# Two spacer tiles of a hybrid-layer kernel made 32 bytes smaller

## The chip, the cores and the metric

The kernel runs on one core of one Trainium2 chip. The metric is the device time in microseconds. The time before is the median of three runs; profiles are of one execution, whose span (first to last instruction) and own time are given apart.

## The reference

One layer of a streaming encoder on 256 positions of width 2048, in float32. Three sub-layers add to the residual x, each on a modulated RMS norm whose shift, scale and gate come from a vector c:

```python
h = modulate(rms_norm(x, ffn1_norm[l]), sh1, sc1)
x = x + HALF_STEP * g1[:, None, :] * swiglu(h, ffn1_w1[l], ffn1_w3[l], ffn1_w2[l])
h = modulate(rms_norm(x, mix_norm[l]), sh2, sc2)
x = x + g2[:, None, :] * hybrid_mixer(h, w_in[l], ...)
h = modulate(rms_norm(x, ffn2_norm[l]), sh3, sc3)
x = x + HALF_STEP * g3[:, None, :] * swiglu(h, ffn2_w1[l], ffn2_w3[l], ffn2_w2[l])
...
return modulate(rms_norm(x, final_norm), sh_f, sc_f)
```

`swiglu` is `(silu(h @ w1) * (h @ w3)) @ w2` with 5632 hidden columns. `hybrid_mixer` projects h by one matrix of 12,288 columns into a gated convolution branch (31 taps, layer norm), a retention branch (4 heads with q, k of 256 and v of 512 columns, decay, group norm, swish gate) and two gates, and merges the branches. Almost all of the work is matrix products with weights that are each used once.

## The kernel before

Everything is kept transposed: features lie on the 128 partitions, the 256 positions along the free axis. A float32 number is held as two halves in the type float32r, a rounded high half and the low rest. A product of two such numbers is three matmuls: high by high, high by low, low by high. This holds for the weights (tiles `hi` and `lo`) and for the activations (h, s, r2, z, mg2, each with a high and a low half behind one another).

**Weights.** `prep` (L178 to L198) loads a block of up to 1 MB into one of four buffers `raw` by a DMA on SyncE's queue. ScalarE copies a half block into `hi` (L189, five buffers), VectorE subtracts to get `lo` (L192, five buffers). `gemm` (L206 to L219) then runs the products of an output tile: for each 128 x 128 block of weights, which is the stationary operand, one matmul of 256 columns with the high half of the activation and one with the low half (L216, `ps<-h,hi` where h is the moving operand), and after those of a half block the low weights by the high activation (L218). Each matmul has its own weight load, which TensorE carries out while the matmul before it runs. Where six banks are filled side by side (the first part of each feed-forward block and of the mixer), `mm3` (L200 to L204) does the same block by block on three lines. Only `value` (L523 to L538) turns this round: there a 128-column slice of h is stationary, and 512 columns of `hi` or `lo` are the moving operand.

**Order of the work.** First feed-forward block: 24 of 44 hidden tiles with h as the moving operand, in four sets, while h is still being made (L390 to L418); then the rest by `ffn` (L342): a stretch with h as the moving operand, then one with the hidden activations s (`s2` tiles), twice over. Then the mixer: q, k and convolution tiles from h, four heads, each with scores, outputs and `value`; then the gates, W_o with r2 as the moving operand, the pointwise convolution with z, the merged projection with mg2. Then the second feed-forward block. Between the parts a norm needs the whole of x, so TensorE pauses. VectorE also reduces the modulation rows (L110) between the weights.

**Where tiles lie.** Tiles of a pool lie behind one another in each partition's memory, in the order in which their names first come up. Pool `keep` comes first, with h at its start, then pool `wp` with `raw`, the weight halves and the spacers, then the pools of the stages. `apart` (L92 to L96) makes a tile of a given number of bytes once per name, and GpSimd clears it; nothing reads it. The spacers are `apart_w` (L187, 64 bytes) between `raw` and `hi`, `apart_s` (L191, 192 bytes) behind `lo`, and in the mixer's first pool `apart_k` (L579, 64 bytes) between q and k and `apart_p` (L551, 192 bytes) between v and p.

All blocks of `hi`, `lo`, h and the other activations are multiples of 512 bytes long, so what is left of an address modulo 256 is set by the spacers and a few small tiles. From the start of h to `hi` there are 99,136 bytes (h 32,768; the vectors 2176; x 16,384; ones 512; cb 8192; small tiles 704, 128, 256, 32 and 32; ssq 2048; three tiles of 1024; `raw` 32,768; `apart_w` 64), which is 64 modulo 256: h lies 192 beyond `hi` and `lo`. The five buffers of `hi`, the five of `lo` and `apart_s` take 40,960 + 192 bytes, so what begins behind them (s, z, r2, mg2, q) lies 192 beyond `hi` as well. k lies 64 beyond q, so q lies 192 beyond k; p lies 192 beyond v. In `value`, where the operands change places, the moving `hi` lies 64 beyond the stationary h.

In front of each product, then, the moving operand's address is 192 more than the stationary one's, modulo 256, except in `value`.

Of the kernel before, what the change touches and what calls it, by code (L numbers as in the profile page):

```python
# [52 lines left out]
def hybrid_layer(ctx, tc, xT, c, vecs, rope, decay, adaT, w13, w13s, w13t, mixs, w2g, w_ab, w_qk, w_v, w_g,  # L53
# [7 lines left out]
    wp = ctx.enter_context(tc.tile_pool(name="wp", bufs=1))  # L61
# [30 lines left out]
    def apart(pool, name, n):  # L92

        if name not in set_apart:
            set_apart.add(name)
            nc.gpsimd.memset(pool.tile([P, n // 4], F32, name=name, tag=name, bufs=1), 0.0)  # L96
# [3 lines left out]
    def raw_load(src, n):  # L100
        r = wp.tile([P, 2048], F32, name="raw", tag="raw", bufs=RAW)
        nc.sync.dma_start(r[:, :n], src)
        return r
# [49 lines left out]
    def tick():  # L153
        ada_done()
        credit[0] += rate["ada"]
        if credit[0] >= 1.0:
            credit[0] -= 1.0
            ada_ahead()
        taps_credit[0] += rate["taps"]
        while taps_credit[0] >= 1.0:  # L160
            taps_credit[0] -= 1.0
            if taps:
                taps.pop(0)()
        due = []
        for e in later:
            e[0] -= 1
            if e[0] <= 0:
                due.append(e)
        for e in due:
            later.remove(e)  # L170
            e[1]()
# [6 lines left out]
    def prep(src, nk, w, ticks=True):  # L178

        n = nk * w  # L180
        r = raw_load(src, n)
        hk = (nk + 1) // 2
        got = []
        for k0 in range(0, nk, hk):
            k1 = min(nk, k0 + hk)
            c0, c1 = k0 * w, k1 * w
            apart(wp, "apart_w", 64)  # L187
            hi = wp.tile([P, 1024], F32R, name="hi", tag="hi", bufs=HI)
            A.copy(hi[:, :c1 - c0], r[:, c0:c1])  # L189
            lo = wp.tile([P, 1024], F32R, name="lo", tag="lo", bufs=LO)  # L190
            apart(wp, "apart_s", 192)  # L191
            V.tensor_tensor(lo[:, :c1 - c0], r[:, c0:c1], hi[:, :c1 - c0].bitcast(F32), op=ALU.subtract)  # L192
            for k in range(k0, k1):
                b = slice((k - k0) * w, (k - k0 + 1) * w)
                got.append((hi[:, b], lo[:, b], hi))
        if ticks:
            tick()
        return got  # L198
# [126 lines left out]
    def side_by_side(srcs, h, ks, banks, ticks=True):  # L325

        for i, k in enumerate(ks):
            w = prep(srcs[k], 2 * S0, P, ticks)
            across(w, h[k], banks, i == 0, i == len(ks) - 1)
# [12 lines left out]
    def ffn(pool, i, h, s, store):  # L342

        f0 = 0
        for g, n in enumerate(GROUPS):
            last = g == len(GROUPS) - 1
            for f in range(f0 + len(s), f0 + n):
                ps = pair([lambda u=u: prep(w13[i, u, f], ND, P) for u in range(2)], h)
                s.append(hidden(pool, two(ps)))
            st = Stream(pool, half_g[:, i])  # L350
            cuts = [0, n] if n <= ND else [0, n // 2, n]
            for t in range(0, ND, 2):
                if last and t == ND - 4:
                    table(AF.Abs_reciprocal_sqrt)
                    ada_until(9 if i else 3)
                    ada_done()
                    rate["ada"] = 0.0
                ada_until(8 if i else 2, t + 1)
                if last:
                    ada_until(10 if i else 4, t + 1)  # L360
                ps = pair([lambda u=u: [e for a, b in zip(cuts, cuts[1:])
                                        for e in prep(w2g[i][g][t + u, :, a * P:b * P], b - a, P)]
                           for u in range(2)], s)
                st.add(t, ps, last, last and store)
            f0 += n
            s = []
        return st
# [401 lines left out]
```

## Time and profile before

| | |
|---|---|
| median of 3 runs | 2292.61 us (2267.69 to 2320.36) |
| the profiled execution's own time | 2288.67 us |
| its span | 2286.9 us |
| mean granted TensorE clock | 0.995 |
| read from HBM | 609.77 MB, 268 GB/s over the span (with what is written) |
| instructions | 44,559 |

In the lines of the profile, PE is TensorE's matmuls, PEld its weight loads, DVE VectorE, ACT ScalarE, POOL GpSimd. A group's line gives the line of the kernel, the engine and the operation, the tile written and the tiles read, the shape and the count, then the busy time in us, the mean duration of one in ns, and the idle time of the engine in front of them with what ended it. Matmuls overlap, so a duration of 277 ns does not mean that one begins every 277 ns. A row of the table of stretches gives the stretch in us, its length, the time TensorE was busy in it with the number of matmuls that touch it, the granted clock, the DMA engines' busy share and GB/s. A row of the timeline gives start, duration, and in brackets the idle time ahead with what ended it.

### The profile page before, as it was taken

Reading aid. Unit: us, or ns where it says so; the run is one execution under the profiler, and the core shown is the slowest. Engines: PE = TensorE matmul, PEld = TensorE weight load, DVE = VectorE, ACT = ScalarE, POOL = GpSimd, SP = SyncE. Lnnn points to the kernel's source line nnn. Section 1 sums busy time; section 2 is a strip of 40 time slices with the busy share of each in tenths; the row PEclk is TensorE's granted clock in tenths of the full one; section 3 lists DMA queues with packets and bytes.
Section 4 is the critical chain, followed back from the end, with each engine's and each line's share of the span. In section 5 each row is a group of like instructions: output and inputs, shape, how many; then the busy total and the mean of one; then the engine's idle time right before and its main releaser. Section 6 shows DMA issues by size and latency. Waiting matters only on the chain.

```text
span 2286.9 us, 44559 instructions
## 1 busy us (share of the span) xinstructions
PE 2248.2 (98%) x19036; PEld 2221.7 (97%) x19036; DVE 1760.4 (77%) x2212; ACT 1067.3 (47%) x1367; POOL 0.6 (0%) x8
## 2 busy tenths in 40 slices
PE   7999999999999999999999999999999999999997
PEld 5999999999999999999999999999999999999997
DVE  7899887778778669898998788777766666666664
ACT  6544653334444644545544644446544443344443
POOL 0000000000000000000000000000000000000000
PEclk9999999999999999999999999999999999999999
DMA  9999689989888465555777698976877777777762
GB/s 344 349 330 326 221 293 319 332 329 349 311 320 330 155 226 204 175 176 180 253 258 273 224 349 321 339 278 230 292 260 257 269 255 268 272 275 266 250 250 83
DMA packets 92217, 616.86 MB, mean 270 GB/s; under 512 B 10225, under 2 KB 10481, under 8 KB 34673
## 3 DMA queue, kind: packets, MB, share of 16 engines
q1 hardware_dynamic: 90290, 609.81, 74.1%
q10 hardware_dynamic: 1728, 4.20, 0.5%
q8 instruction: 149, 2.44, 0.4%
q14 instruction: 50, 0.41, 0.0%
HBM read 609.77 MB, written 4.19 MB: 268 GB/s over the span
## 4 chain that ended last, share of the span: by engine, by line
PE 95%; DVE 2%; DMA 1%; ACT 1%; issue 0%; DVEq 0%; ACTq 0%
PE ps L216 50%; PE ps L218 25%; PE ps L202 7%; PE ps L203 7%; PE ps L204 6%; DMA raw<-in_adaT 1%; DMA raw<-in_w13s 1%; DVE lo L192 0%; DVE raw L110 0%; DVE f L671 0%; DVE part L416 0%; DVE ssq L272 0%; ACT hi L189 0%; ACT L245 0%; ACT L238 0%
## 5 line engine op out<-in xcount | busy, mean ns | idle before, releaser
L189 ACT CAST hi<-raw 128x1024 fp32r<-128x1024 f32 (+2 forms) x864 | 843.9, 986 | 1116.3 <-PE ps L216 595.4
L192 DVE TENSOR_TENSOR lo<-raw,hi 128x1024 fp32r<-128x1024 f32 (+2 forms) x864 | 978.5, 1142 | 450.0 <-ACT hi L189 429.6
L216 PE MATMUL ps<-h,hi 128*128 128x256 f32 x5888 | 733.5, 277 | 0.0
L216 PEld LDWEIGHTS ps<-h,hi 128*128 128x128 f32 x5888 | 700.3, 188 | 0.2
L110 DVE CUSTOM_DVE_ANT_0 raw<-raw,cb,vec 128x2048 f32<-128x2048 f32 x176 | 412.6, 2345 | 2.6 <-DMA raw<-in_adaT 2.6
L218 PE MATMUL ps<-h,lo 128*128 128x256 f32 x2944 | 396.4, 277 | 0.0
L218 PEld LDWEIGHTS ps<-h,lo 128*128 128x128 f32 x2944 | 363.8, 188 | 0.0
L216 PE MATMUL ps<-s,hi 128*128 128x256 f32 x2816 | 356.7, 279 | 0.0
L216 PEld LDWEIGHTS ps<-s,hi 128*128 128x128 f32 x2816 | 339.3, 188 | 0.0
L202 PE MATMUL ps<-h,hi 128*128 128x256 f32 x1152 | 315.0, 281 | 14.0 <-ACT h L305 13.8
L203 PE MATMUL ps<-h,hi 128*128 128x256 f32 x1152 | 319.9, 280 | 3.9 <-DVE h L308 3.9
L204 PE MATMUL ps<-h,lo 128*128 128x256 f32 x1152 | 317.1, 280 | 0.0
L202 PEld LDWEIGHTS ps<-h,hi 128*128 128x128 f32 x1152 | 216.5, 191 | 16.1 <-ACT h L305 15.3
L203 PEld LDWEIGHTS ps<-h,hi 128*128 128x128 f32 x1152 | 219.8, 191 | 4.5 <-DVE h L308 4.4
L204 PEld LDWEIGHTS ps<-h,lo 128*128 128x128 f32 x1152 | 218.9, 191 | 0.0
L218 PE MATMUL ps<-s,lo 128*128 128x256 f32 x1408 | 193.9, 279 | 0.0
L218 PEld LDWEIGHTS ps<-s,lo 128*128 128x128 f32 x1408 | 176.9, 189 | 0.0
L443 DVE SCALAR_TENSOR_TENSOR acc<-y,vec,acc 128x256 f32<-128x256 f32 x240 | 114.0, 480 | 2.7
L216 PE MATMUL ps<-r,hi 128*128 128x256 f32 x512 | 63.6, 276 | 0.0
L216 PE MATMUL ps<-mg,hi 128*128 128x256 f32 x512 | 63.4, 276 | 0.0
L216 PEld LDWEIGHTS ps<-r,hi 128*128 128x128 f32 x512 | 60.5, 188 | 0.0
L216 PEld LDWEIGHTS ps<-mg,hi 128*128 128x128 f32 x512 | 60.5, 188 | 0.0
(152 smaller groups left out, 1171.6 us busy)
## 6 DMA issues: line engine op xcount, KB each, us to landing
raw<-in_adaT SPq DMA_DIRECT2D x176, 1024.0 KB, 5.9
raw<-in_w SPq DMA_DIRECT2D x148, 1024.0 KB, 5.6
raw<-in_w SPq DMA_DIRECT2D x64, 896.0 KB, 5.7
raw<-in_w13s SPq DMA_DIRECT2D x64, 768.0 KB, 6.1
raw<-in_w_v SPq DMA_DIRECT2D x16, 1024.0 KB, 4.8
raw<-in_w_g SPq DMA_DIRECT2D x16, 1024.0 KB, 4.9
raw<-in_w_gr SPq DMA_DIRECT2D x16, 1024.0 KB, 5.0
raw<-in_w_o SPq DMA_DIRECT2D x16, 1024.0 KB, 5.2
```

The costliest lines, as they stand in the source:

```text
L110: tc.keep_in_program_order(V.tensor_tensor_reduce(r, r, cb, 1.0, vec[:, b:b + 1], op0=ALU.mult, op1=ALU.add, accum_out=mod[:, j, t:t + 1]))
L189: A.copy(hi[:, :c1 - c0], r[:, c0:c1])
L192: V.tensor_tensor(lo[:, :c1 - c0], r[:, c0:c1], hi[:, :c1 - c0].bitcast(F32), op=ALU.subtract)
L202: PE.matmul(o, st[0], mv[0], start=start, stop=False, skip_group_check=skip)
L203: PE.matmul(o, st[0], mv[1], start=False, stop=False, skip_group_check=skip)
L204: PE.matmul(o, st[1], mv[0], start=False, stop=stop, skip_group_check=skip)
L216: PE.matmul(o, w[k][0], mv[k][:, half], start=k == 0 and half == 0, stop=False)
L218: PE.matmul(o, w[k][1], mv[k][:, 0], start=False, stop=k == n - 1)
L443: tc.keep_in_program_order(V.scalar_tensor_tensor(out=acc[:, t], in0=y[:, t, k:k + T], scalar=vec[:, dw + k:dw + k + 1], in1=acc[:, t], op ...
```

## The change

Two spacers become 32 bytes smaller:

```diff
-            apart(wp, "apart_w", 64)
+            apart(wp, "apart_w", 32)
             hi = wp.tile([P, 1024], F32R, name="hi", tag="hi", bufs=HI)
             A.copy(hi[:, :c1 - c0], r[:, c0:c1])
             lo = wp.tile([P, 1024], F32R, name="lo", tag="lo", bufs=LO)
-            apart(wp, "apart_s", 192)
+            apart(wp, "apart_s", 160)
```

`hi` and `lo` move down by 32 bytes and everything behind `apart_s` by 64. h stays: it now lies 224 bytes beyond the weights' halves, modulo 256. s, z, r2, mg2 and q lie 160 beyond them. In `value` the moving `hi` lies 32 beyond the stationary h. q and k, and v and p, move together, and their 192 stays. No instruction is added or taken away.

## The prediction

> **What bounds the kernel now.** I read the page's busy line first, then the chain that ended last, then the costliest groups.
>
> ```profile
> PE 2248.2 (98%) x19036; PEld 2221.7 (97%) x19036; DVE 1760.4 (77%) x2212; ACT 1067.3 (47%) x1367; POOL 0.6 (0%) x8
> ...
> PE 95%; DVE 2%; DMA 1%; ACT 1%; issue 0%; DVEq 0%; ACTq 0%
> ...
> L189 ACT CAST hi<-raw 128x1024 fp32r<-128x1024 f32 (+2 forms) x864 | 843.9, 986 | 1116.3 <-PE ps L216 595.4
> L192 DVE TENSOR_TENSOR lo<-raw,hi 128x1024 fp32r<-128x1024 f32 (+2 forms) x864 | 978.5, 1142 | 450.0 <-ACT hi L189 429.6
> ```
>
> TensorE is busy 98% of the span and holds 95% of the chain. The two halvings that feed it (L189, L192) wait for it, ACT for 595.4 us on L216 alone. So TensorE's stream of weight load and matmul sets the end, and what counts is its pace: the time from one matmul's start to the next.
>
> The second question is which matmuls meet which spacing. These are the groups by line:
>
> ```profile
> L216 PE MATMUL ps<-h,hi 128*128 128x256 f32 x5888 | 733.5, 277 | 0.0
> ...
> L218 PE MATMUL ps<-h,lo 128*128 128x256 f32 x2944 | 396.4, 277 | 0.0
> ...
> L216 PE MATMUL ps<-s,hi 128*128 128x256 f32 x2816 | 356.7, 279 | 0.0
> ...
> L203 PE MATMUL ps<-h,hi 128*128 128x256 f32 x1152 | 319.9, 280 | 3.9 <-DVE h L308 3.9
> L204 PE MATMUL ps<-h,lo 128*128 128x256 f32 x1152 | 317.1, 280 | 0.0
> L202 PE MATMUL ps<-h,hi 128*128 128x256 f32 x1152 | 315.0, 281 | 14.0 <-ACT h L305 13.8 <-ACT h L311 0.2
> ...
> L218 PE MATMUL ps<-s,lo 128*128 128x256 f32 x1408 | 193.9, 279 | 0.0
> ...
> L216 PE MATMUL ps<-r,hi 128*128 128x256 f32 x512 | 63.6, 276 | 0.0
> L216 PE MATMUL ps<-mg,hi 128*128 128x256 f32 x512 | 63.4, 276 | 0.0
> ...
> L203 PE MATMUL ps<-lo,h 128*128 128x512 f32 x128 | 50.8, 397 | 0.0
> ```
>
> With moving operand h: 5888 + 2944 + 3 x 1152 = 12,288. With s: 2816 + 1408 = 4224; r and mg 768 each (512 and half as many lo), z 384: together 6144. So 18,432 matmuls of 256 columns change their spacing. The value projection is apart: 3 x 128 = 384 matmuls of 512 columns, h stationary and hi or lo moving.
>
> The third view is the one that decides: how many matmuls fall into a stretch without idle time, by stage.
>
> ```profile
> core 0: us, PE busy (x), PEclk, DMA share, GB/s
> 100.00:225.00 125.00, 125.00 (x1105) 1.00 0.91 330
> 227.00:337.00 110.00, 110.00 (x936) 1.00 0.73 253
> 341.00:495.00 154.00, 154.00 (x1309) 1.00 0.91 327
> ...
> 782.00:842.00 60.00, 60.00 (x532) 1.00 0.66 220
> 846.00:864.00 18.00, 18.00 (x80) 1.00 0.64 225
> ...
> 1460.00:1540.00 80.00, 80.00 (x708) 1.00 0.85 312
> 1600.00:1840.00 240.00, 240.00 (x2120) 1.00 0.75 268
> 1880.00:2000.00 120.00, 120.00 (x1062) 1.00 0.77 273
> ```
>
> A matmul that straddles an edge is counted, so I take two off each count (one or two for the 512-column row). 100 to 225 us gives 125,000/1103 = 113.3 ns; 1600 to 1840 gives 113.3; s from 1880 gives 113.2; mg from 1460 gives 113.3. But 227 to 337, also h, gives 110,000/934 = 117.8 ns, and s from 341 gives 117.8. The granted clock is 1.00 in all of them. **There are two paces for the same instruction, shape and spacing: 113.3 and 117.8 ns.** I call them the lower and the upper rung. What moves the stream from one to the other is in the timeline:
>
> ```profile
> 225.75 0.28 PE L204 MATMUL ps<-h,lo 128*128 128x256 f32 x1
> 226.25 0.39 PE L202 MATMUL ps<-h,hi 128*128 128x256 f32 x1 [0.22 <-ACT h L311]
> ```
>
> One stall of a fraction of a microsecond, and the upper rung stands from there through h, s, h and s until the next pause:
>
> ```profile
> core 0: us, PE busy (x), PEclk, DMA share, GB/s
> 227.00:768.00 541.00, 541.00 (x4595) 1.00 0.84 306
> ...
> 1280.00:1543.00 263.00, 263.00 (x2323) 1.00 0.85 312
> 1557.00:2270.00 713.00, 713.00 (x6294) 1.00 0.71 255
> ```
>
> The DMA share is 0.84 on the upper rung and 0.91 or 0.71 on the lower, so neither clock nor DMA load is the cause; what the rows leave is how the weight load's reads and the moving operand's reads fall relative to each other. That is a reading of these rows, not something that one of them shows directly.
>
> From the rungs follow two fixed points. The 4593 matmuls of the upper stretch cost 4.5 ns each over the lower rung, 21 us: a run wholly on the lower rung would be 2288.7 - 21 = 2268 us, and the fastest of the three runs is 2267.69. All 18,432 on the upper rung would be 2268 + 83 = 2351; the slowest run, 2320.36, lies between. The spread of before is then about which rung a run falls on. My sums start from the profiled execution (span 2286.9, its time 2288.67), which is 4 us under the median of 2292.61.
>
> **The change part by part.** Two memsets get shorter:
>
> ```profile
> L96 POOL MEMSET apart_w<- x1: 111/111/111, 0.7 to 0.7; 128x16 f32 x1
> L96 POOL MEMSET apart_s<- x1: 138/138/138, 0.8 to 0.8; 128x48 f32 x1
> ```
>
> They run in the first microsecond on an engine busy for 0.6 us in all, before TensorE has an operand; if nothing hid them they would be worth under 0.3 us. No instruction, transfer or wait is added or removed, and no buffer count changes. Everything rests on addresses.
>
> ACT's and DVE's tiles shift too, in 864 copies and 864 subtractions. The rows of L189 and L192 bound this: ACT waits 1116 us and DVE 450 us ahead of them, so even 10% on each (84 and 98 us) stays inside that slack. I take 0.
>
> Not touched are the head's own products: k sits behind its spacer of 64 and p behind its spacer of 192, both unchanged, so q against k and p against v keep their 192.
>
> For the rest no row shows a matmul at 224 or 160. The nearest rows are the spacing 192 itself, and the value projection, whose moving hi lies 64 beyond its stationary h. The row from 846 to 864 gives 18,000/78.5 = 229 ns for 512 columns. To compare, I need what 256 columns cost when nothing is held up. The nearest is a weight load whose neighbour has no matmul streaming yet:
>
> ```profile
> 33.73 0.19 PEld L203 LDWEIGHTS ps<-h,hi 128*128 128x128 f32 x1 [1.33 <-DVE h L308]
> 33.84 0.19 PEld L204 LDWEIGHTS ps<-h,lo 128*128 128x128 f32 x1
> 33.96 0.19 PEld L202 LDWEIGHTS ps<-h,hi 128*128 128x128 f32 x1
> ```
>
> The first gap is 0.11 us, the next, with matmuls running, 0.12. I take 110 ns as the unheld pace of load and 256 columns (an estimate; the view rounds to 10 ns). A 512-column matmul at 64 is then held for 229 - 220 = 9 ns, a 256-column one at 192 for 114.4 on average (3.3 or 7.8 by rung, a quarter of the matmuls on the upper) - 110 = 4.4. So spacing matters, and 64 is the worse by 4.7 ns a matmul.
>
> On a circle of 256 bytes, 192 and 64 are opposite; 224 and 160 both lie 32 of 128 bytes on the way from the one to the other. My value is a quarter of the difference, 1.2 ns on each of 18,432 matmuls, +22 us: **2288.7 + 22 = 2311 us**. In terms of rungs it says that half of the matmuls run on the upper instead of a quarter. The bounds: never held, -4.4 ns (-81 us); as badly held as at 64, +4.7 ns (+87 us); the class with h twice as heavy as the other. The value projection goes from 64 to 32: 384 matmuls, between all its hold gone (-3 us) and as much again (+3); I take 0, as both ends are small.
>
> A rule of the Trainium skill speaks against any effect. "TensorE: Matmul & The Clock Gate", section "Part 2: What happens when you issue a matmul", gives TensorE two independent read ports and says that loading the next weights takes nothing from the running matmul. By it, the sum would be 0 and the time 2289. The two paces at one clock do not bear it out as it stands, though they do not show the ports either.
>
> **The rivals.**
>
> *Nothing happens* (the paces do not depend on a 32-byte shift): rungs and odds as now, 2289 us, anywhere from 2268 to 2320. For it: 4593 matmuls in a row stayed on one rung through changes of tile, slot and load. Against it: 229 ns at spacing 64. The same holds if spacers are rounded up to a coarser grain when memory is laid out, since the change would then not do what it says. The port rule of the Trainium skill above is this case too.
>
> *Slower: a third rung becomes the standing one.* One matmul shows it:
>
> ```profile
> 1556.27 0.29 PE L204 MATMUL ps<-h,lo 128*128 128x256 f32 x1
> 1556.40 0.28 PE L202 MATMUL ps<-h,hi 128*128 128x256 f32 x1
> ```
>
> Here the gap is 0.13 us, about one step above the upper rung (117.8 + 4.5 = 122 ns, an estimate that fits the row). If h at 224 locks there, 12,288 x (122 - 114.4) = 93 us: 2382 us; s, r, mg and z at 160 alone would add 47 (2336), both 140 (2429). A hold as at 64 for all gives 2376, so I price the case at 2380. It decides from a mean pace of 117.1 ns on (2338 us). For it: the rungs are evenly spaced, and the next one is visited. Against: at 192 it is left at once.
>
> *Faster: the reads stop meeting.* All at 110 ns: 2288.7 - 81 = 2208 us; h alone -54 (2235), the 160 class alone -27 (2262). For it: the bare load shows that the floor is there, 3.3 ns under the lower rung. Against: no long stretch of the trace stands on it.
>
> **How the numbers follow.** Forecast 0.36, with its own range 2268 to 2351; nothing happens 0.14; slower 0.32; faster 0.18. A measurement of this kernel tells about 2% from no change: below 2247 or above 2338. Of the forecast 0.04 lies above 2338; of the faster case 0.02 (the 160 class alone) lies within. So faster 0.16, same 0.32 + 0.14 + 0.02 = 0.48, slower 0.32 + 0.04 = 0.36. The range goes from all reads apart, 2208, rounded to 2205, to a little above the slower case's 2380, at 2400; both classes on the third rung (2429) is left out.
>
> **What would show it right or wrong.** The stretches of the table, counted again, should give paces between 113 and 118 ns, h and s stretches not alike, and the same clock; L216 on h should have a mean above 277 ns if its share of the upper rung grows. The value projection should move by a few ns from 229. All of it is wrong if stages without idle time show paces of 110 ns or under, or of 122 and over, for a whole stage; if the paces are unchanged but idle time ahead of PE grows (over the 14.0 and 3.9 us of L202 and L203), the address story itself is wrong, and the feeding engines were the ones that changed.

## The result and the profile after

The changed kernel takes 2356.2 us (median of 4 runs, 2355.19 to 2356.44) against 2306.49 for the kernel before in the same comparison (4 runs, 2267.69 to 2322.88): a ratio of 1.0305, 95% interval 1.025 to 1.036. The ratio goes by fast runs alone, without those of before that lie more than 1.5% above its fastest; the plain medians are 2.2% apart. It is slower: its fastest run lies above every run of before, here and in the comparisons below. It is also steadier: its four runs lie within 1.3 us, those of before within 55.

The page of the changed kernel, the lines that answer to those shown of before (its span is 2353.4 us, the profiled execution's time 2355.19):

```profile
PE 2315.4 (98%) x19036; PEld 2287.5 (97%) x19036; DVE 1764.5 (75%) x2212; ACT 1071.4 (46%) x1367; POOL 0.6 (0%) x8
...
PE 97%; DVE 1%; ACT 1%; issue 0%; DVEq 0%
...
L189 ACT CAST hi<-raw 128x1024 fp32r<-128x1024 f32 (+2 forms) x864 | 846.6, 986 | 1183.0 <-PE ps L216 728.3
L192 DVE TENSOR_TENSOR lo<-raw,hi 128x1024 fp32r<-128x1024 f32 (+2 forms) x864 | 981.1, 1143 | 503.6 <-ACT hi L189 485.7
L216 PE MATMUL ps<-h,hi 128*128 128x256 f32 x5888 | 757.1, 281 | 0.0
...
L202 PE MATMUL ps<-h,hi 128*128 128x256 f32 x1152 | 319.2, 285 | 13.8 <-ACT h L305 13.8
L203 PE MATMUL ps<-h,hi 128*128 128x256 f32 x1152 | 324.1, 284 | 3.5 <-DVE h L308 3.5
```

The instruction counts are the same. One ScalarE copy takes 986 ns as before, one subtraction 1143 against 1142; ScalarE waits longer, for TensorE above all (L216, 728.3 us against 595.4), and VectorE behind it. TensorE's idle time (span less busy) is 38.0 us against 38.7. All of the 66.5 us is in TensorE's busy time: the same matmuls follow one another more slowly. The mean duration of L216 on h went from 277 to 281 ns.

The table of stretches of the changed kernel, each stretch with one class of matmul and no idle time (in this order: h, s, h, value, mg, h, s, h, s):

```profile
core 0: us, PE busy (x), PEclk, DMA share, GB/s
35.00:346.00 311.00, 311.00 (x2626) 1.00 0.84 300
349.00:504.00 155.00, 155.00 (x1324) 1.00 0.91 333
507.00:685.00 178.00, 178.00 (x1506) 1.00 0.87 321
...
856.00:875.00 19.00, 19.00 (x83) 1.00 0.63 218
...
1493.00:1580.00 87.00, 87.00 (x744) 1.00 0.80 296
1589.00:1906.00 317.00, 317.00 (x2674) 1.00 0.71 255
1909.00:2063.00 154.00, 154.00 (x1315) 1.00 0.75 265
2066.00:2245.00 179.00, 179.00 (x1515) 1.00 0.71 252
2248.00:2336.00 88.00, 88.00 (x744) 1.00 0.44 152
```

And three stretches of the kernel before with nearly the same counts (mg, h, s):

```profile
1459.00:1543.00 84.00, 84.00 (x744) 1.00 0.83 307
1552.00:1856.00 304.00, 304.00 (x2667) 0.99 0.74 264
...
2186.00:2270.00 84.00, 84.00 (x744) 1.00 0.44 158
```

Two off each count again for the edges. With h at 224 the pace is 118.3 ns (178,000/1504 = 118.4, 179,000/1513 = 118.3; the two longer stretches, which begin just behind a pause, give 118.5 and 118.6). Neither 113.3 nor 117.8 is left. With the rest at 160 there are two paces: 117.3 (349 to 504, 1493 to 1580, 1909 to 2063) and 118.7 (the last, 88,000/742 = 118.6). The last row of both shows the loss plainly: 744 matmuls of s in 84 us before, 88 after, at the same clock and the same DMA share. The value projection goes from 229 to 19,000/81.5 = 233 ns.

Over all 18,432 matmuls the mean pace went from 114.4 to 118.1 ns: 3.7 x 18,432 = 68 us, and 384 x 4 ns = 2 us in the value projection, against 66.5 measured; a tenth of a nanosecond in the paces is 2 us.

### The profile page after: what moved, and what is told of

It reads as the page before. It is cut to its first block, busy times and chain, and to the rows that moved or that the text cites. A ratio compares the mean times of both kernels' runs of the same rounds, so it can differ in the third digit from the quotient of the medians.

```text
span 2353.4 us, 44559 instructions
## 1 busy us (share of the span) xinstructions
PE 2315.4 (98%) x19036; PEld 2287.5 (97%) x19036; DVE 1764.5 (75%) x2212; ACT 1071.4 (46%) x1367; POOL 0.6 (0%) x8
## 4 chain that ended last, share of the span: by engine, by line
PE 97%; DVE 1%; ACT 1%; issue 0%; DVEq 0%
PE ps L216 50%; PE ps L218 25%; PE ps L202 7%; PE ps L203 7%; PE ps L204 7%; DVE f L671 0%; DVE ssq L272 0%; ACT L245 0%; ACT L238 0%; DVE lo L192 0%; PE gn_v L256 0%; PE gn_m L256 0%; DVE raw L110 0%; ACT sq L288 0%; PE r L256 0%
## 5 line engine op out<-in xcount | busy, mean ns | idle before, releaser
L189 ACT CAST hi<-raw 128x1024 fp32r<-128x1024 f32 (+2 forms) x864 | 846.6, 986 | 1183.0 <-PE ps L216 728.3
L192 DVE TENSOR_TENSOR lo<-raw,hi 128x1024 fp32r<-128x1024 f32 (+2 forms) x864 | 981.1, 1143 | 503.6 <-ACT hi L189 485.7
L216 PE MATMUL ps<-h,hi 128*128 128x256 f32 x5888 | 757.1, 281 | 0.0
L216 PEld LDWEIGHTS ps<-h,hi 128*128 128x128 f32 x5888 | 722.4, 188 | 0.2
L218 PE MATMUL ps<-h,lo 128*128 128x256 f32 x2944 | 408.2, 281 | 0.0
L218 PEld LDWEIGHTS ps<-h,lo 128*128 128x128 f32 x2944 | 373.8, 188 | 0.0
L216 PE MATMUL ps<-s,hi 128*128 128x256 f32 x2816 | 362.2, 280 | 0.0
L216 PEld LDWEIGHTS ps<-s,hi 128*128 128x128 f32 x2816 | 344.6, 188 | 0.0
L202 PE MATMUL ps<-h,hi 128*128 128x256 f32 x1152 | 319.2, 285 | 13.8 <-ACT h L305 13.8
L203 PE MATMUL ps<-h,hi 128*128 128x256 f32 x1152 | 324.1, 284 | 3.5 <-DVE h L308 3.5
L204 PE MATMUL ps<-h,lo 128*128 128x256 f32 x1152 | 321.0, 283 | 0.0
L202 PEld LDWEIGHTS ps<-h,hi 128*128 128x128 f32 x1152 | 217.1, 192 | 15.5 <-ACT h L305 15.3
L203 PEld LDWEIGHTS ps<-h,hi 128*128 128x128 f32 x1152 | 219.9, 191 | 4.2 <-DVE h L308 4.0
L204 PEld LDWEIGHTS ps<-h,lo 128*128 128x128 f32 x1152 | 218.4, 191 | 0.0
L216 PE MATMUL ps<-r,hi 128*128 128x256 f32 x512 | 66.2, 281 | 0.0
L216 PE MATMUL ps<-mg,hi 128*128 128x256 f32 x512 | 65.4, 280 | 0.0
L216 PEld LDWEIGHTS ps<-r,hi 128*128 128x128 f32 x512 | 63.0, 189 | 0.0
L216 PEld LDWEIGHTS ps<-mg,hi 128*128 128x128 f32 x512 | 62.4, 188 | 0.0
```

The source lines that it names most:

```text
L202: PE.matmul(o, st[0], mv[0], start=start, stop=False, skip_group_check=skip)
L203: PE.matmul(o, st[0], mv[1], start=False, stop=False, skip_group_check=skip)
L204: PE.matmul(o, st[1], mv[0], start=False, stop=stop, skip_group_check=skip)
L216: PE.matmul(o, w[k][0], mv[k][:, half], start=k == 0 and half == 0, stop=False)
L218: PE.matmul(o, w[k][1], mv[k][:, 0], start=False, stop=k == n - 1)
```

## The experiments

### Each part alone, the parts swapped, everything moved

**h at 224 alone.** Only the first spacer shrinks.

```diff
-            apart(wp, "apart_w", 64)
+            apart(wp, "apart_w", 32)
```

> apart_w 32 and apart_s 192: h 224 beyond the weights' halves, everything behind apart_s back at 192. If the spacing of a product's two operands sets its pace (theory S): stages with h at 118.3 ns a matmul as after the change, stages with s, r2, z and mg2 on the two rungs of before (113.3 or 117.8 ns); time 2268 + 12288 x 5.0 ns = 2329 us with the rest on the lower rung, up to 2357 on the upper. If the place of the weights' halves itself is what counts (theory P: they lie where they lie after the change): both classes as after, 2353 us, s at 117.4.

2340.97 us (4 runs); ratio to before 1.0243, interval 1.017 to 1.0316 (before in this and the next three: 2280.98, 19 runs, 2267.14 to 2321.21). Its stretches of h, s, s:

```profile
35.00:346.00 311.00, 311.00 (x2626) 1.00 0.84 300
349.00:504.00 155.00, 155.00 (x1319) 1.00 0.91 325
...
689.00:773.00 84.00, 84.00 (x744) 1.00 0.83 302
```

h has the row of the changed kernel to the last digit. s, back at 192, shows both rungs of before, 117.7 and 113.2 ns. The halves lie where they lie after the change, and s does not mind: it is the spacing, not the place.

**The rest at 160 alone.**

```diff
-            apart(wp, "apart_s", 192)
+            apart(wp, "apart_s", 160)
```

> apart_w 64 and apart_s 160: h at 192, the rest at 160. Theory S: h stages at 113.3 or 117.8 ns by chance, s, r2, z and mg2 at 117.3 to 118.5 whatever the rung before them; time 2268 + 6144 x 4.3 ns = 2294 us with h wholly on the lower rung, up to 2349. Theory P (the halves lie as before the change): both classes on the two rungs, 2268 to 2350 with stretches of 113.3 in s stages.

2307.91 us (10 runs); 1.011, interval 1.0065 to 1.0155. Stretches of h, s, h, s:

```profile
507.00:685.00 178.00, 178.00 (x1514) 1.00 0.87 322
688.00:776.00 88.00, 88.00 (x744) 1.00 0.79 288
...
2039.00:2210.00 171.00, 171.00 (x1511) 1.00 0.73 262
2213.00:2300.00 87.00, 87.00 (x743) 1.00 0.43 151
```

h at 192 is on the upper rung (117.7) in the first pair and on the lower (113.3) in the second, and s follows: 118.6 after the upper, 117.4 after the lower. So s at 160 also has two paces, both above 117, and in this run they go with the rung that h leaves. That is not all that decides: in the changed kernel both paces of s stand behind h at 118.3. The parts alone cost 60 and 27 us over that median, both together 75 (2356.2, from the comparison further up, less 2281); they need not add, since before itself scatters between rungs.

**Spacings swapped.**

```diff
-            apart(wp, "apart_w", 64)
+            apart(wp, "apart_w", 96)
...
-            apart(wp, "apart_s", 192)
+            apart(wp, "apart_s", 224)
```

> apart_w 96 and apart_s 224: the spacings change places, h at 160, the rest at 224. Theory S: h stages at about 117.4 ns, the others at about 118.4; time 2268 + 12288 x 4.1 + 6144 x 5.1 ns = 2350 us. If instead the stage or the tile decides (theory T: something about h and its order of use): h stages stay at 118.3 and s at 117.4, 2355 us. The paces tell these apart, the times do not.

2356.27 us (4 runs); 1.0313, interval 1.0239 to 1.0387. Stretches of h and s:

```profile
506.00:683.00 177.00, 177.00 (x1511) 1.00 0.87 324
...
2244.00:2332.00 88.00, 88.00 (x746) 1.00 0.43 153
```

h now runs at 117.3 and s at 118.3 in its 744: the paces went with the spacings, not with the tiles.

**Everything moved, spacings kept.** The addresses modulo 256 of the halves are those of the changed kernel.

```diff
+    nc.gpsimd.memset(sb(keep, [P, 56], "apart_h"), 0.0)
     crow = sb(keep, [1, D], "crow", tag="h")
```

> Spacers as before, and a new tile of 224 bytes in front of h: every tile moves by 224, the halves lie where they lie after the change modulo 256, all spacings stay 192. Theory S: nothing changes, paces 113.3 or 117.8 ns by chance, 2268 to 2350 us. Theory P: paces and time as after the change, 118.3 and 117.4 ns, 2353 us.

2288.27 us (10 runs); 1.0005, interval 0.9953 to 1.0058. Stretches of s and h:

```profile
346.00:501.00 155.00, 155.00 (x1318) 1.00 0.93 335
...
1556.00:1860.00 304.00, 304.00 (x2671) 0.99 0.74 265
```

117.8, and 113.9 in a stretch whose granted clock is 0.99: the rungs of before. The place alone does nothing.

### The other spacings

**All at 64.**

```diff
-            apart(wp, "apart_w", 64)
+            apart(wp, "apart_w", 192)
...
-            apart(wp, "apart_s", 192)
+            apart(wp, "apart_s", 64)
```

> apart_w 192 and apart_s 64: every class at 64, the opposite of 192 on a circle of 256 bytes. If the hold has a period of 256 bytes and 64 is its worst place (theory S256, the prediction's circle, built on the value projection's 229 ns): about 119 ns a matmul everywhere, 2268 + 18432 x 5.7 ns = 2373 us. If its period is 128 bytes (theory S128: 64 is the same as 192; the value projection measured 229 at 64 and 232 at 32 and 96, so 64 was its best place): the rungs of before, 113.3 or 117.8 ns, 2268 to 2350 us.

2342.89 us (2 runs); 1.0196, interval 1.014 to 1.0252. Stretches of the value projection, h, h, s:

```profile
850.00:870.00 20.00, 20.00 (x88) 1.00 0.64 214
874.00:936.00 62.00, 62.00 (x549) 1.00 0.58 198
...
2054.00:2232.00 178.00, 178.00 (x1514) 1.00 0.70 254
2235.00:2323.00 88.00, 88.00 (x749) 1.00 0.43 152
```

h has 113.3 (62,000/547) and, mostly, 117.7: the rungs of 192, with other odds as far as two runs tell. 119 nowhere. And the value projection, whose operands now lie 192 apart, needs 231 ns by this short row (20,000/86.5) and 233.3 as the mean over all of it, where that mean is 229.1 at 64.

**h at 96, the rest at 32; h at 128, the rest at 0.** `apart_w` is 160 and `apart_s` 32 in the first, 128 and 256 in the second.

> apart_w 160 and apart_s 32: h at 96, the rest at 32. S128: h as at 224 (118.3 ns, one pace only), the rest as at 160 (117.3 or 118.7 ns), 2353 us, the changed kernel again. S256: both three quarters of the way from 192 to 64, somewhat under the pace at 64 and alike.

> apart_w 128 and apart_s 256: h at 128, the rest at 0. S128: both classes share their paces; whether above 118 ns, where no run has been yet, or not, is open, my guess from 192, 160 and 224 is about 120 ns (one more step of half the distance), 2268 + 18432 x 6.7 = 2391 us. S256: the two lie alike at half way between 192 and 64, 116 to 117 ns, 2320 to 2340 us.

2372.51 us (1.0325, 1.0269 to 1.038) and 2377.21 us (1.0345, 1.0289 to 1.0401), 2 runs each. The first kernel's stretches of h, s and s, then the second's of h and s:

```profile
353.00:508.00 155.00, 155.00 (x1319) 1.00 0.91 325
512.00:693.00 181.00, 181.00 (x1511) 1.00 0.87 321
...
2267.00:2353.00 86.00, 86.00 (x739) 1.00 0.44 153
```

```profile
515.00:694.00 179.00, 179.00 (x1511) 1.00 0.87 320
697.00:786.00 89.00, 89.00 (x744) 1.00 0.78 286
```

96 has 120.0 (181,000/1509), not the 118.3 of 224; 32 has 117.8 and 116.7, not the paces of 160; 128 has 118.6 (and 120.1 in an earlier stretch), 0 has 120. So a period of 128 bytes falls too, although 64 and 192 share their rungs, and so does an even slope over 256.

**Half steps and smaller.** h can be read from a few bytes into its tile; two of the three kernels give it another place in each of its three lives.

```diff
-        return sb(keep, [P, ND, 2, T], "h", F32R)
+        j = h_at.pop(0)
+        return sb(keep, [P, 2 * ND * T + 8], "h", F32R)[:, j:j + 2 * ND * T].rearrange("p (n u t) -> p n u t", n=ND, u=2)
```

> h is read from 16 bytes into its tile and apart_w is 32, apart_s 192: h at 208, half a spacer step from 192 towards 224, the rest at 192. If the hold grows evenly with the distance from 192: h between 113.3 or 117.8 and 118.3, about 116 ns. If it goes by steps of 32 bytes: h at 118.3 as at 224, or at the rungs of 192. Faster than 113.3 would say that 192 isn't the best place: at 110 ns, 2268 - 12288 x 3.3 = 2227 us.

> h is read from a few bytes into its tile, another place in each of its three lives, with apart_w 64 and apart_s 192: h at 184 in the first feed-forward block, at 176 in the mixer, at 188 in the second block; the rest at 192. If the paces go by 32-byte steps: 117.3 or 118.7 as at 160, or the rungs of 192, in all three. If they go by steps of 16 bytes (208 was neither 192 nor 224): 176 unlike 184 and 188, and those two the rungs of 192 (113.3 or 117.8). If every 4 bytes count: three paces; 110 ns is the floor that I would expect, 117 the likeliest for 176.

> As the run before with apart_w 32: h at 200 in the first feed-forward block, at 216 in the mixer, at 196 in the second block; the rest at 192. By 16-byte steps: 200 and 196 the rungs of 192 (113.3 or 117.8), 216 the 119.2 of 208. If every 4 bytes count: three paces between those of 192 and 224, 114 to 119 ns.

2339.79 us (2 runs, 1.0182, 1.0128 to 1.0237), 2342.86 and 2378.29 us (one run each, before 2307.25 beside them). Stretches of h at 208 and of s at 192 in the first kernel; h at 184, 176 and 188 in the second; at 200, 216 and 196 in the third:

```profile
504.00:684.00 180.00, 180.00 (x1512) 1.00 0.89 331
687.00:771.00 84.00, 84.00 (x743) 1.00 0.82 302
```

```profile
506.00:687.00 181.00, 181.00 (x1510) 1.00 0.87 324
...
877.00:942.00 65.00, 65.00 (x547) 1.00 0.54 187
...
2056.00:2237.00 181.00, 181.00 (x1514) 1.00 0.69 249
```

```profile
506.00:688.00 182.00, 182.00 (x1515) 1.00 0.86 322
...
878.00:945.00 67.00, 67.00 (x557) 1.00 0.53 185
...
2084.00:2269.00 185.00, 185.00 (x1515) 1.00 0.68 244
```

208: 119.2 ns. 184: 120.0; 176: 119.3; 188: 119.7. 200: 120.3; 216: 120.7; 196: 122.3. Four bytes from 192 is the worst place found. By steps of 16 bytes the rungs of 192 should have stood at 196 and 200; they don't.

One thing is not separated here. In these three kernels, and in no other, h is read from a place in its tile that is no multiple of 32 bytes, so this place may count and not the spacing: 16 bytes into its tile h ran at 119.2 (spacing 208) and 119.3 (176), 24 bytes into it at 120.0 (184) and 120.7 (216). The spacings also count the longer tile of h as rounded up to a multiple of 32 bytes, as the 4-byte tiles are in the sum for the kernel before.

All paces of 256-column matmuls, from the stretches above and before:

| moving operand beyond the stationary, bytes modulo 256 | ns a matmul |
|---|---|
| 0 | 120.0 |
| 32 | 116.7 or 117.8 |
| 64 | 113.3 or 117.8 |
| 96 | 120.0 |
| 128 | 118.6 or 120.1 |
| 160 | 117.3 or 118.7 |
| 176, 184, 188 (h off a multiple of 32 in its tile) | 119.3, 120.0, 119.7 |
| 192 | 113.3 or 117.8 |
| 196, 200, 208, 216 (the same) | 122.3, 120.3, 119.2, 120.7 |
| 224 | 118.3 |

### What reads against what

**Nearly no halving.** The changed kernel's spacings, but `prep` hands out five kept pairs of blocks in turn:

```diff
+        if not kept:
...
+                kept.append((hi, lo))
...
-        r = raw_load(src, n)
...
+            hi, lo = kept[turn[0] % HI]
+            turn[0] += 1
```

> The changed kernel's spacings (h 224, the rest 160), but only five blocks of weights are loaded and halved, once at the start, and every product reuses them; nearly all weight DMAs and all other halvings of ScalarE and VectorE are left out, so the output isn't the layer's. If the pace comes from TensorE's own two reads, the weight load's and the moving operand's (theory S): h stages stay at 118.3 ns, s, r2, z and mg2 at 117.3 or 118.7, and the time goes down only by what PE waits for weights. If ScalarE's and VectorE's reads and writes of the same memory, or the DMAs, cost the time (theory T, traffic): paces fall to 113 ns or under, 2270 us or less.

2360.71 us (one run). The page's busy line, and the stretches of h, mg and, last, s:

```profile
PE 2316.9 (98%) x19036; PEld 2289.2 (97%) x19036; DVE 855.4 (36%) x1353; ACT 255.2 (11%) x508; POOL 0.6 (0%) x8
```

```profile
511.00:689.00 178.00, 178.00 (x1507) 1.00 0.36 131
...
1497.00:1584.00 87.00, 87.00 (x744) 1.00 0.37 134
...
2254.00:2342.00 88.00, 88.00 (x744) 1.00 0.00 1
```

ACT went from 46% to 11%, DVE from 75% to 36%, the DMA share in the first row from 0.87 to 0.36, and 1507 matmuls of h still need 178 us, 744 of mg still 87. In the last row the DMA share is 0.00, VectorE is busy for 14.85 of the 88 us and ScalarE for 4.43, and s needs what it needed in the changed kernel. So the other engines' traffic is not what sets the pace. What is left is TensorE's own reading: its weight loads and its moving operand.

**Low weights at 0, high weights at 192.**

```diff
+            apart(wp, "apart_l", 192)
             lo = wp.tile([P, 1024], F32R, name="lo", tag="lo", bufs=LO)
-            apart(wp, "apart_s", 192)
+            apart(wp, "apart_s", 256)
```

> A third spacer of 192 bytes between hi and lo: every moving operand stays 192 beyond the high halves and lies 0 beyond the low halves (0 had 120.0 ns in the run with h at 128). In L202 to L204 one matmul of three has low weights. If a matmul is held while the next one's weights are loaded beside it (theory N): the gap from the start of L203's matmul to that of L204's is the long one, about 120 ns, the two others 113 to 118. If a matmul is held by the place of its own weights (theory O): the gap from L204 to the next L202 or L203 is the long one. Both: a mean pace a third of the way from 113.3 or 117.8 to 120, that is 115.6 to 118.5 ns, 2268 + 18432 x 2.3 to 5.2 = 2310 to 2364 us. If the gaps are alike in all three places, the pace is set over several matmuls and this run does not tell N from O.

2357.79 us (4 runs); 1.0334, interval 1.0254 to 1.0414. Its timeline in the first feed-forward block (the lines are one further down, so L205 has the low weights):

```profile
100.45 0.28 PE L203 MATMUL ps<-h,hi 128*128 128x256 f32 x1
100.57 0.28 PE L204 MATMUL ps<-h,hi 128*128 128x256 f32 x1
100.69 0.28 PE L205 MATMUL ps<-h,lo 128*128 128x256 f32 x1
100.80 0.28 PE L203 MATMUL ps<-h,hi 128*128 128x256 f32 x1
```

The gaps are alike, three in 0.35 us or 117 ns each, so where high and low weights alternate this run does not say whether a matmul meets the next one's weight load or its own. It says something else: one badly placed matmul in three is enough to take the lower rung away from all three. In `gemm`, where they stand in groups, the same trace says more (here L217 has the high weights, L219 the low):

```profile
561.28 1.12 PE L219 MATMUL ps<-h,lo 128*128 128x256 f32 x8
562.24 2.05 PE L217 MATMUL ps<-h,hi 128*128 128x256 f32 x16
564.12 1.12 PE L219 MATMUL ps<-h,lo 128*128 128x256 f32 x8
565.08 1.11 PE L217 MATMUL ps<-h,hi 128*128 128x256 f32 x8
```

From start to start, eight matmuls with low weights take 0.96 us, 120 ns each, and sixteen with high weights 1.88 us, 117.5 each. The pace of 0 and the upper rung of 192 stand side by side, group by group. From 507 to 686 us the starts in the trace, taken to the nanosecond, are 119.6 ns apart between two low-weight matmuls and 117.8 between two with high weights. From the last low one to the next high one it is 117.7, from the last high one to the next low one 118.7 (63 of each). The gap behind the last low one is not long, which speaks for the load that runs beside a matmul (theory N) and against the matmul's own weights (theory O). But 118.7 lies half way, so N is not shown.

## Why the prediction was right and wrong

**Right: where the time is.** TensorE's pace sets the end, and nothing but addresses changed: idle time, ScalarE, VectorE and the memsets count for nothing, as priced. The two rungs hold, and the reading of the spread fits: over the 19 runs beside the first four experiments the kernel before reached 2267.14 at best, where the sum said 2268 for the lower rung alone, and stayed under the 2351 of the upper. No run near either end was profiled, so this reading is not shown.

**Wrong: the size, and so the forecast of no change.** The step that failed is "My value is a quarter of the difference, 1.2 ns on each of 18,432 matmuls, +22 us". Measured is 3.7 ns, and 66.5 us. Two things under that step were wrong. The first is "64 is the worse by 4.7 ns": I had taken the 229 ns of a 512-column matmul, with the operands' places changed, for a measure of what 64 does to 256 columns. At 64 those run at 113.3 or 117.8, as at 192, and the value projection itself needs 232.6 to 234.2 ns at 32, 96, 128, 160 and 192 (means over all of it): of these places 64 is its best. The second is the even way round the circle: 96 and 0 are at 120.0, with 64 between them at 113.3 or 117.8. There was no slope to interpolate on. The forecast's sign came from 64 being the worse place, so that the time did go up owes to luck.

**Wrong: "half of the matmuls run on the upper instead of a quarter".** The rungs of 192 did not change their odds; at 224 and 160 they are gone, and others stand there. The sign named for it, a mean of L216 on h above 277 ns, came (281) for that other reason. The own range of the forecast, to 2351, missed the result by 5 us; the full range held it.

**The slower case** is the one that came, from the point on that it named (a mean pace over 117.1; measured 118.1), but by another rung. I had priced one more step, 122 ns, for h; 118.3 at 224 is half a nanosecond over the upper rung of 192. 2380 was too much by 24 us.

**Nothing happens** fell with the result, and the first two experiments tie it to the spacing. The Trainium skill's rule from "TensorE: Matmul & The Clock Gate", section "Part 2: What happens when you issue a matmul", that loading the next tile's weights takes no read bandwidth from the running matmul, gives no reason for the operands' places to count, and here they do: at 224 and 160 the paces stay above 117 ns with ScalarE busy 11% and VectorE 36%, and at 192 the lower rung of 113.3 stands under full traffic. Whether read bandwidth is what is lost, no run shows.

**Faster:** no spacing tried reached 110 ns, or a pace clearly below the lower rung. The spacing of before is the best one found; 64 alone shows the same lower rung, and no version beats the kernel before.

**What stays open.** Why 64 and 192 have the low rung, and what sets which rung a restart falls on (a wait of a fraction of a microsecond is enough, and the stage ahead passes its rung on), was not settled. That the weight load that matters is the one running beside the matmul is likely, by the groups of the last run, but not shown. Whether the fine places count by spacing or by where in its tile h starts is open, and places within 32 bytes of 64 were not tried.

## What to carry to other kernels

Where matmuls of 256 columns each have their own weight load and stand back to back, count the matmuls in a stretch without idle time: two paces for one instruction at one clock were here the sign that the spacing of the operands in memory costs time, and a spacer between the two operands' tiles, 32 bytes longer or shorter, was worth 3%. One in front of both did nothing. Don't interpolate between spacings, and don't carry the finding from one shape to another: measure each. And when a kernel's runs scatter by 2%, look for such rungs before judging a change by one run of each.

## What the runs showed of the hardware

A fine dependence on address that no view names: 32 bytes of spacing took the pace of h from 113.3 or 117.8 to 118.3 ns, and 4 bytes, by spacing or by h's place in its tile, to 122.3, at a granted clock of 1.00. A lock that lasts: 4593 matmuls in a row stayed at 117.8 ns in the profile before, through stages and DMA loads, where 113.3 was possible, until a pause. And a rung that passes from one operand to the next: with h at 192, s at 160 ran at 118.6 behind h on its upper rung and at 117.4 behind h on its lower.
